# The first norm's factors: from column sums and a trip through memory to Newton steps on a row and 32x32 transpositions

## The chip, the cores and the metric

The kernel runs on one core of a Trainium2 chip. The metric is the device time of one execution in microseconds; the median of three runs is used. Times inside an execution come from the hardware profiler and count from the first instruction (the span).

## The reference

Two layers of a decoder trunk are computed for 256 new prompt tokens and for 8 sample sequences of 8 tokens: T = 320 tokens of D = 1024 features, in float32. Every sub-layer starts with an RMS norm. What the change touches is the norm of the first sub-layer and its two readers, the halves u and v of the first projection:

```
def rmsnorm(x, g):
    x32 = x.astype(jnp.float32)
    y = x32 * lax.rsqrt(jnp.mean(x32 * x32, axis=-1, keepdims=True) + EPS)
    return (y * g.astype(jnp.float32)).astype(x.dtype)

h = rmsnorm(x, norm_mix_g[0])
...
    h = jax.nn.gelu(x @ w_in)          # x is the normed input, (T, 1024) @ (1024, 4096)
    u, v = jnp.split(h, 2, axis=-1)    # 2048 columns each
    ... layer norm of v over its columns, spatial gating of v in chunks of 128 tokens ...
    y = (u * mixed.reshape(bsz, s, D_A)) @ w_out
```

## The kernel before

**Layout.** Activations lie with features on the 128 partitions and tokens along the row (xT: 8 blocks of 128 features x 320 tokens). Each float32 operand of a large matmul is split in a high part of reduced precision and the rest (xh and xl, wh and wl), and three matmuls (high by high, high by low, low by high) give the product. Weights come by DMA into raw; ScalarE copies raw to wh (L181), VectorE subtracts to get wl (L182). Both have three buffers, so the split of a group of weights may run as soon as TensorE has left the group three before it. A group here is two blocks of 128 rows by 512 columns, 16 matmuls of 512 columns.

**The norm's factor.** A norm's factor of a token is one over the root of the mean square. The kernel multiplies by the norm's weights g ahead of the matmuls (norm_block), and by the factor behind them: the factor is needed only where the product is read.

**v first.** layer_a starts with v in four passes (q = 0 to 3) over 512 columns each. In a pass the tokens are the rows of the result: pv[0] and pv[1] hold the two prompt halves of 128 tokens, pvs the 64 sample tokens. pv comes from the PSUM pool psa (five banks of 128x512), pvs from the pool psm (three). v_gelu(q, pv) reads a pass: for each token half ScalarE applies GELU with the factor as a scale per partition (L457; column t of self.rc), VectorE takes statistics (L458); the sample tokens are first summed from two halves of pvs (L454, L455) and then treated alike (L459, L460). After pass 0 the squares of x are summed over the 8 blocks into acc, 128x320 (square_block, L238 to L242). In pass 1, after four of eight blocks, norm_cols() gives the factors as columns (token on the partition, self.rc is 128x3), and v_gelu(0) follows; v_gelu(1) stands at the end of pass 1.

**norm_cols.** Each 128 tokens of acc are multiplied by ones, two columns wide (tile pc); VectorE scales and adds EPS (ms, L267), GpSimd raises to the power -0.5 (rc, L268).

**The row.** u is computed after v, with tokens along the row, and is multiplied by the factors as a row that is the same on all partitions (self.rb, L557). Before the change this row is got through memory: GpSimd writes self.rc into the array sums in DRAM (L477); later one DMA brings sums back to all partitions (back_a), together with row sums of the spatial weights (row_sums, L407 to L409: GpSimd masks wn, VectorE reduces it to rs8, DMA to sums). sums_laid then has ScalarE copy the row into self.rb (norm_back, L282 and L283), and GpSimd lay out rsum (L418).

**A norm that stands in the kernel already.** The norms ahead of the two gated MLPs use norm_spread and norm_root: acc is split, two matmuls with ones (128x128) add it up over the partitions and leave the sum on all of them (tile pb, 128x320), and eleven VectorE operations on 128x320 make the factors: half (L321), a first guess by integer arithmetic (L322) and three Newton steps of three operations (L324 to L326).

**Order.** TensorE's instructions stay in program order. On the other engines the order is fixed when the kernel is built, by a list scheduler that takes what is ready; each engine then runs its instructions strictly in that order.

Of the kernel before, what the change touches and what calls it, by code (L numbers as in the profile page):

```python
# [10 lines left out]
F32 = mybir.dt.float32  # L11
# [6 lines left out]
P = 128  # L18
EPS = 1e-6
TINY = 1e-37  # L20
TP = 256
NB, NS = 8, 8
T = TP + NB * NS
# [4 lines left out]
NH = 8  # L28
DK = 128
DV = 256  # L30
# [10 lines left out]
class Net:  # L41
# [232 lines left out]
        self.nc.scalar.copy(self.spread(acc2), self.twice(self.acc[:, TP:]))  # L274
        return acc2

    def norm_back(self, rows):

        nc = self.nc
        rows = rows.rearrange("p (c t) -> p t c", t=3)  # L280
        self.rb = self.tp.tile([P, T], F32, tag="rb", name="rb", bufs=1)
        nc.scalar.copy(self.rb[:, :TP].rearrange("p (t c) -> p t c", c=P), rows[:, :2, :])  # L282
        nc.scalar.copy(self.rb[:, TP:], rows[:, 2, 64:])  # L283

    def norm_row(self):

# [85 lines left out]
    def layer_a(self):  # L372
        nc, tc, I, O = self.nc, self.tc, self.I, self.O
        with tc.tile_pool(name="ya", bufs=1) as yp, tc.tile_pool(name="la", bufs=1) as lp:
            yh = yp.tile([P, KA, T], F32R, name="yh_a")
            yl = yp.tile([P, KA, T], F32R, name="yl_a")
            v = lp.tile([P, 3, DA], F32, name="v_a")
# [5 lines left out]
            rsum = lp.tile([P, NH, P], F32, name="rs_a")  # L383
            wn = lp.tile([P, NH, P], F32, name="wn_a")
            rs8 = lp.tile([P, NH], F32, name="rs8_a")
# [5 lines left out]
            def load_ws():  # L391
                nc.sync.dma_start(ws, I["a_ws"])
                nc.sync.dma_start(wn, I["a_wsn"])
                nc.sync.dma_start(trit, I["trit"])
                nc.gpsimd.memset(wss, 0.0)
                for r, c in halves:
                    nc.sync.dma_start(wss[r, :, c], I["a_wss"])
                    nc.sync.dma_start(bdt[r], I["bdt"])
                nc.sync.dma_start(bs, I["a_bs"].to_broadcast([P, NH, P]))
                nc.sync.dma_start(self.wg, I["b_wg"])  # L400
                nc.gpsimd.tensor_tensor(self.wg, self.wg, self.xv[:, V_MIX + 8:V_MIX + 16].unsqueeze(2).to_broadcast([P, KD, 32]), op=MULT)
                nc.gpsimd.tensor_tensor(ws, ws, trit.unsqueeze(1).to_broadcast([P, NH, P]), op=MULT)
                for r, c in halves:
                    nc.gpsimd.tensor_tensor(wss[r, :, c], wss[r, :, c], bdt[r].unsqueeze(1).to_broadcast([64, NH, 64]), op=MULT)

            def row_sums():
                nc.gpsimd.affine_select(wn, wn, pattern=[[0, NH], [-1, P]], compare_op=ALU.is_ge, fill=0.0, base=0, channel_multiplier=1)  # L407
                nc.vector.tensor_reduce(rs8, wn, axis=mybir.AxisListType.X, op=ADD)
                nc.gpsimd.dma_start(I["sums"][:, 3 * P:].rearrange("o (t g) -> t (o g)", g=NH), rs8)  # L409

            def sums_back():
                back = lp.tile([P, 11 * P], F32, name="back_a")
                nc.gpsimd.dma_start(back, I["sums"].to_broadcast([P, 11 * P]))
                return back

            def sums_laid(back):
                self.norm_back(back[:, :3 * P])
                nc.gpsimd.tensor_copy(rsum, back[:, 3 * P:].rearrange("p (t g) -> p g t", g=NH))  # L418

            nc.gpsimd.memset(mv[:64, 2, :], 0.0)  # L420

# [15 lines left out]
            def columns(q, k, pv, wh, wl):  # L437

                if q == 0 and k < 2:
                    return first_rows(k, pv, wh, wl)  # L440
                xs = self.xx[:, k, TP:TP + P]
                for t in range(2):
                    xh, xl = self.tokens(self.xh[:, k, :], t), self.tokens(self.xl[:, k, :], t)
                    self.mm(pv[t], xh, wh, k == 0, False)
                    self.mm(pv[t], xl, wh, False, False)
                    self.mm(pv[t], xh, wl, False, k == KD - 1)
                self.mm(pv[2], xs, wh, k == 0, False)
                self.mm(pv[2], xs, wl, False, k == KD - 1)

            def v_gelu(q, pv):  # L450
                cs = slice(q * 512, (q + 1) * 512)
                r = slice(64, P)
                vs = lp.tile([P, 512], F32, tag="vs", name="vs", bufs=2)[r]
                nc.scalar.copy(vs, pv[2][:64])  # L454
                nc.vector.tensor_tensor(vs, vs, pv[2][r], op=ADD)  # L455
                for t in range(2):
                    nc.scalar.activation(v[:, t, cs], pv[t], AF.Gelu_apprx_tanh, scale=self.rc[:, t:t + 1])  # L457
                    nc.vector.bn_stats(st[:, t, q, :], v[:, t, cs])  # L458
                done = nc.scalar.activation(v[r, 2, cs], vs, AF.Gelu_apprx_tanh, scale=self.rc[r, 2:3])  # L459
                return done, nc.vector.bn_stats(st[r, 2, q, :], v[r, 2, cs])  # L460

            waiting = None
            for q in range(4):
                pv = [self.psa.tile([P, 512], F32, tag="pa", name="pv") for _ in range(2)] + \
                    [self.psm.tile([P, 512], F32, tag="pm", name="pvs")]
                k = 0
                while k < KD:
                    (wh, wl), kn = self.take()
                    wh, wl = [x.rearrange("p (k e) c -> p k (e c)", e=4) for x in (wh, wl)]
                    for i in range(kn):  # L470
                        if q == 0 and k + i + 1 < KD:
                            self.enter(k + i + 1)
                        columns(q, k + i, pv, wh[:, i, :], wl[:, i, :])
                    k += kn
                    if q == 1 and k == 4:
                        self.norm_cols()
                        nc.gpsimd.dma_start(I["sums"][:, :3 * P].rearrange("o (c t) -> c (o t)", t=3), self.rc)  # L477
                        v_gelu(0, waiting)
                    if q == 3 and k == 2:
                        gone = v_gelu(2, waiting)  # L480
                        with self.behind(*gone):
                            sums_laid(back)
                if q == 0:
                    with tc.issue_after(self.last_split.ins):
                        for m in range(KD):
                            self.square_block(m)
                if q == 1:
                    load_ws()
                if q == 2:
                    row_sums()  # L490
                if q == 2:
                    back = sums_back()
                if q in (1, 3):
                    v_gelu(q, pv)
                waiting = pv
# [56 lines left out]
            for b in range(16):  # L552
# [3 lines left out]
                t = lp.tile([P, T], F32, tag="ur", name="ur", bufs=2)  # L556
# [1058 lines left out]
```

## Time and profile before

| | us |
|---|---|
| median of three runs (930.15 to 930.83) | 930.79 |
| the profiled execution | 930.84 |
| its span | 929.1 |
| TensorE busy (matmul) | 923.3 |
| VectorE busy | 692.3 |
| ScalarE busy | 507.5 |
| GpSimd busy | 113.1 |

The four passes of v take about the first 64 us of the span, and u the following 65. In the lines of the timeline the first two numbers are start and duration in us, then come the engine, the line of the kernel, the operation, what is written and what is read with shapes, and in brackets the idle time of the engine before it with what ended it. PE is TensorE's matmul, DVE VectorE, ACT ScalarE, POOL GpSimd.

### The profile page before, as it was taken

How to read it: one execution, taken by the hardware profiler on the slowest of the kernel's cores; microseconds unless marked ns; L12 is line 12 of the kernel's file. 1: busy time of each engine (PE TensorE's matmuls, PEld its weight loads, DVE VectorE, ACT ScalarE, POOL GpSimd, SP SyncE). 2: the span in 40 equal slices, each digit the busy share in tenths (PEclk: the TensorE clock that was granted, in tenths of full speed). 3: DMA queues.
4: the chain of work that ended last, by engine and by line, in shares of the span. 5: the costliest groups of instructions: out<-in, count | busy, mean ns of one | idle time of the engine just before them, and what ended most of it. 6: DMA issues, size and time to landing. Idle time of an engine off the chain costs nothing.

```text
span 929.1 us, 16828 instructions
## 1 busy us (share of the span) xinstructions
PE 923.3 (99%) x6268; PEld 894.2 (96%) x6268; DVE 692.3 (75%) x1299; ACT 507.5 (55%) x892; POOL 113.1 (12%) x312
## 2 busy tenths in 40 slices
PE   9999999999999999999999999999999999999997
PEld 8889999999999999998998989989999999999997
DVE  6667985597777764458999999798889777775551
ACT  7458544355544543336777786575655544544341
POOL 2400000011000000103221211001002110100001
PEclk9999999999999999999999999999999999999999
DMA  8866444444444445447688778775474444445642
GB/s 284 262 170 174 139 143 151 145 152 148 155 148 148 151 147 157 151 153 221 198 255 263 241 256 265 216 249 175 156 231 146 150 156 141 154 141 154 210 147 69
DMA packets 70625, 166.61 MB, mean 179 GB/s; under 512 B 12416, under 2 KB 31112, under 8 KB 70544
## 3 DMA queue, kind: packets, MB, share of 16 engines
q1 hardware_dynamic: 70336, 164.82, 56.9%
q8 instruction: 49, 0.80, 0.3%
q0 software_dynamic: 208, 0.73, 0.2%
q14 instruction: 32, 0.26, 0.1%
HBM read 149.20 MB, written 16.32 MB: 178 GB/s over the span
## 4 chain that ended last, share of the span: by engine, by line
PE 99%; DVEq 0%; DVE 0%; issue 0%
PE pm L50 78%; PE pv L50 10%; PE pvs L50 3%; PE num L50 2%; PE pyt L50 1%; PE pmix L50 1%; PE py L50 1%; PE psc L50 1%; PE pCp L50 1%; PE pcs L50 1%; PE pw L50 0%; PE pk L53 0%; PE pg L50 0%; PE pc L50 0%; PE pb L50 0%; PE pMb L50 0%
## 5 line engine op out<-in xcount | busy, mean ns | idle before, releaser
L181 ACT CAST wh<-raw 128x1024 fp32r<-128x1024 f32 (+4 forms) x252 | 254.8, 1012 | 278.4 <-PE pm L50 147.4
L182 DVE TENSOR_TENSOR wl<-raw,wh 128x1024 fp32r<-128x1024 f32 (+4 forms) x252 | 298.1, 1183 | 110.9 <-ACT wh L181 108.6
L50 PE MATMUL pm<-xh,wh 128*128 128x320 f32 x1088 | 338.3, 311 | 0.0
L50 PE MATMUL pm<-xh,wl 128*128 128x320 f32 x1088 | 336.2, 309 | 0.0
L50 PE MATMUL pm<-xl,wh 128*128 128x320 f32 x1088 | 336.1, 309 | 0.0
L50 PEld LDWEIGHTS pm<-xh,wh 128*128 128x128 f32 x1088 | 204.3, 188 | 1.7 <-ACT wh L181 0.5
L50 PEld LDWEIGHTS pm<-xl,wh 128*128 128x128 f32 x1088 | 204.3, 188 | 0.2
L50 PEld LDWEIGHTS pm<-xh,wl 128*128 128x128 f32 x1088 | 204.3, 188 | 0.0
L50 PE MATMUL pm<-yl_f,wh 128*128 128x320 f32 x308 | 95.1, 309 | 0.0
L50 PE MATMUL pm<-yh_f,wh 128*128 128x320 f32 x308 | 95.1, 309 | 0.0
L50 PE MATMUL pm<-yh_f,wl 128*128 128x320 f32 x308 | 95.1, 309 | 0.0
L50 PEld LDWEIGHTS pm<-yh_f,wl 128*128 128x128 f32 x308 | 57.9, 188 | 0.0
L50 PEld LDWEIGHTS pm<-yh_f,wh 128*128 128x128 f32 x308 | 57.9, 188 | 0.0
L50 PEld LDWEIGHTS pm<-yl_f,wh 128*128 128x128 f32 x308 | 57.9, 188 | 0.0
L602 DVE SCALAR_TENSOR_TENSOR fcv<-fpad,vecs,fcv 128x336 f32<-128x336 f32 x88 | 49.7, 564 | 1.5
L50 PE MATMUL pv<-wh,xh 128*128 128x512 f32 (+1 forms) x132 | 50.6, 389 | 0.0
L50 PE MATMUL pv<-wh,xl 128*128 128x512 f32 (+1 forms) x132 | 50.4, 387 | 0.0
L50 PE MATMUL pv<-wl,xh 128*128 128x512 f32 (+1 forms) x132 | 50.2, 386 | 0.0
L347 DVE TENSOR_TENSOR xT<-pm,xT 128x320 f32<-128x320 f32 x38 | 18.5, 489 | 30.5 <-PE pm L50 30.5
L50 PE MATMUL pm<-yhb,wh 128*128 128x320 f32 x128 | 39.6, 310 | 0.0
L50 PE MATMUL pm<-yh_a,wh 128*128 128x320 f32 x128 | 39.6, 309 | 0.0
L50 PE MATMUL pm<-yh_a,wl 128*128 128x320 f32 x128 | 39.5, 309 | 0.0
(354 smaller groups left out, 1446.2 us busy)
## 6 DMA issues: line engine op xcount, KB each, us to landing
raw<-in_f_up SPq DMA_DIRECT2D x88, 512.0 KB, 3.6
raw<-in_b_win SPq DMA_DIRECT2D x32, 512.0 KB, 4.2
raw<-in_f_dn SPq DMA_DIRECT2D x28, 448.0 KB, 3.4
C<-in_C SPq DMA_DIRECT2D x32, 258.0 KB, 4.7
raw<-in_a_win SPq DMA_DIRECT2D x16, 512.0 KB, 3.7
raw<-in_a_wo SPq DMA_DIRECT2D x16, 512.0 KB, 3.7
raw<-in_b_wv SPq DMA_DIRECT2D x16, 512.0 KB, 3.8
out_Cs<-C SPq DMA_DIRECT2D x32, 256.0 KB, 4.0
```

The lines of the kernel that those rows point to most:

```text
L50: self.pin(self.nc.tensor.matmul(out, lhsT, rhs, start=start, stop=stop))
L181: self.last_split = nc.scalar.copy(wh[:, c, :], raw[:, c, :])
L182: self.last_low = nc.vector.tensor_tensor(wl[:, c, :], raw[:, c, :], wh[:, c, :].bitcast(F32), op=SUB)
L347: self.last_sum = self.nc.vector.tensor_tensor(x, ps[:, :T], x, op=ADD)
L602: nc.vector.scalar_tensor_tensor(cv, pd[:, i:i + NC], self.vec(w + i * KF), cv, op0=MULT, op1=ADD)
```

## The change

norm_cols is no longer called in the first layer. acc is split after pass 0 (norm_spread), and at the place in pass 1 where norm_cols stood, norm_root gives the row of factors self.rb on all partitions. A new function root_cols makes the columns out of it: since the row is the same on every partition, the 32x32 transposition of the block of partitions 32g to 32g+31 and of tokens 32g to 32g+31 has in its first column the factors of these tokens. Six VectorE transpositions do this (for each of four blocks of partitions one for the two prompt halves, and two for the sample tokens). self.rc is then a strided view of the result. The trip of the row through DRAM and norm_back go, and the array sums keeps only the spatial weights' row sums.

```diff
-    def norm_back(self, rows):
-
-        nc = self.nc
-        rows = rows.rearrange("p (c t) -> p t c", t=3)
-        self.rb = self.tp.tile([P, T], F32, tag="rb", name="rb", bufs=1)
-        nc.scalar.copy(self.rb[:, :TP].rearrange("p (t c) -> p t c", c=P), rows[:, :2, :])
-        nc.scalar.copy(self.rb[:, TP:], rows[:, 2, 64:])
+    def root_cols(self):
+
+        cols = self.tp.tile([P, 3, 32], F32, tag="rcols", name="rcols", bufs=1)
+        for g in range(4):
+            r = slice(32 * g, 32 * g + 32)
+            self.nc.vector.transpose(cols[r, :2, :], self.rb[r, :TP].rearrange("p (t c) -> p t c", c=P)[:, :, r])
+            if g > 1:
+                self.nc.vector.transpose(cols[r, 2, :], self.tokens(self.rb[r], 2)[:, r])
+        self.rc = cols[:, :, 0]
...
-                nc.gpsimd.dma_start(I["sums"][:, 3 * P:].rearrange("o (t g) -> t (o g)", g=NH), rs8)
+                nc.gpsimd.dma_start(I["sums"].rearrange("o (t g) -> t (o g)", g=NH), rs8)
...
-                back = lp.tile([P, 11 * P], F32, name="back_a")
-                nc.gpsimd.dma_start(back, I["sums"].to_broadcast([P, 11 * P]))
+                back = lp.tile([P, NH * P], F32, name="back_a")
+                nc.gpsimd.dma_start(back, I["sums"].to_broadcast([P, NH * P]))
...
-                self.norm_back(back[:, :3 * P])
-                nc.gpsimd.tensor_copy(rsum, back[:, 3 * P:].rearrange("p (t g) -> p g t", g=NH))
+                nc.gpsimd.tensor_copy(rsum, back.rearrange("p (t g) -> p g t", g=NH))
...
                     if q == 1 and k == 4:
-                        self.norm_cols()
-                        nc.gpsimd.dma_start(I["sums"][:, :3 * P].rearrange("o (c t) -> c (o t)", t=3), self.rc)
+                        self.norm_root(*parts)
+                        self.root_cols()
                         v_gelu(0, waiting)
...
                         for m in range(KD):
                             self.square_block(m)
+                        parts = self.norm_spread()
```

More of the change, by code (lines that the diff above doesn't have):

```diff
@@ L1597 @@
     O = {k: nc.dram_tensor("out_" + k, s, F32, kind="ExternalOutput").ap() for k, s in _OUTS.items()}
-    for k, v in dict(rows=(8, 456), sums=(1, 11 * P), turn=(NH, P, 3 * DV), kturn=(NH, P, TP), frows=(P, 5 * T)).items():
+    for k, v in dict(rows=(8, 456), sums=(1, NH * P), turn=(NH, P, 3 * DV), kturn=(NH, P, TP), frows=(P, 5 * T)).items():
         I[k] = nc.dram_tensor(k, v, F32, kind="Internal").ap()
```

## The prediction

> **What bounds the kernel now.** I read the page first: its span, and the chain of work that ended last.
>
> ```profile
> span 929.1 us, 16828 instructions
> ...
> PE 99%; DVEq 0%; DVE 0%; issue 0%
> ```
>
> TensorE carries 99% of the chain. A microsecond of VectorE, ScalarE or GpSimd work is therefore worth nothing unless TensorE waits for it, and every wait that is put into TensorE's stream is lost for good. So I asked two things: what the change does to TensorE's own work, and whether something that TensorE needs comes later.
>
> Next I read the timeline of TensorE around the place of the edit (start, duration, then the instruction).
>
> ```profile
> 27.44 0.72 PE L50 MATMUL pc<-ones,acc 128*128 128x2 f32 x6
> 28.02 0.48 PE L50 MATMUL pv<-wh,xh 128*128 128x512 f32 x1
> 28.34 0.40 PE L50 MATMUL pv<-wh,xl 128*128 128x512 f32 x1
> ...
> 35.38 0.39 PE L50 MATMUL pv<-wh,xh 128*128 128x512 f32 x1
> ...
> 36.06 0.39 PE L50 MATMUL pv<-wh,xh 128*128 128x512 f32 x1
> ```
>
> At 27.44 stand the column sums of the norm, in the middle of the second of four passes over the columns of v (q = 1). At 35.38 the third pass (q = 2) begins with the tokens' first half; three matmuls later, at 36.06, it turns to the second half. Three steps in 0.68 us are 0.227 us a matmul of 512 columns: the stream is unbroken. Both times are deadlines. The pool psa has five banks: two hold pass 0, two hold pass 1, and the fifth serves the norm's sum. When pass 2 begins, one bank is free and the other comes back only when v_gelu(0) has read pass 0's first bank. v_gelu(0) needs the norm's factors as columns of tokens (self.rc).
>
> **The change part by part.**
>
> TensorE's own work. Removed are the six rows of pc: from 27.44 to 28.34 stand these and one matmul of v, so they cost 0.90 - 0.23 = 0.67 us. Added are the two matmuls of ones with the split sums of squares. The same two stand in the next layer's norm:
>
> ```profile
> 190.38 0.31 PE L50 MATMUL pb<-acc_h,ones 128*128 128x320 f32 x1
> 190.53 0.31 PE L50 MATMUL pb<-acc_l,ones 128*128 128x320 f32 x1
> 190.68 0.31 PE L50 MATMUL pm<-xh,wh 128*128 128x320 f32 x1
> ```
>
> They hold the stream for 190.68 - 190.38 = 0.30 us. TensorE gains 0.37 us, and the deadlines move to 35.01 (first bank) and 35.69 (second).
>
> VectorE around it, by its timeline:
>
> ```profile
> 25.22 1.23 DVE L182 TENSOR_TENSOR wl<-raw,wh 128x1024 fp32r<-128x1024 f32 x1 [0.29 <-ACT wh L181]
> 28.20 0.16 DVE L267 TENSOR_SCALAR ms<-pc 128x3 f32<-128x3 f32 x1 [1.75 <-PE pc L50]
> ...
> 35.03 1.22 DVE L408 TENSOR_REDUCE rs_a<-wn_a 128x8 f32<-128x1024 f32 x1 [0.99 <-POOL wn_a L407]
> 36.17 1.28 DVE L458 BATCH_NORM_STATS2 st_a<-v_a 128x6 f32<-128x512 f32 x2
> 37.48 0.69 DVE L455 TENSOR_TENSOR vs<-vs,pvs 64x512 f32<-64x512 f32 x1
> ```
>
> and ScalarE's:
>
> ```profile
> 27.41 1.05 ACT L181 CAST wh<-raw 128x1024 fp32r<-128x1024 f32 x1 [2.22 <-PE pvs L50]
> 29.37 1.27 ACT L457 ACTIVATE v_a<-pv,rc 128x512 f32<-128x512 f32 x2 [0.92 <-POOL rc L268]
> ...
> 31.73 1.05 ACT L181 CAST wh<-raw 128x1024 fp32r<-128x1024 f32 x1 [0.34 <-PE pvs L50]
> ...
> 35.84 0.58 ACT L454 COPY vs<-pvs 64x512 f32<-64x512 f32 x1
> ```
>
> Before, the factors are there at 29.37, one VectorE and one GpSimd operation behind the sums, so the first GELU of pass 0 ends at about 30.05 (half of that row), 6.0 us ahead of 36.06. That 6.0 us is all the cover there is for the new chain.
>
> The split of the sums (ScalarE's copy, VectorE's subtraction) goes into idle time: ScalarE is idle for 2.22 us up to 27.41, VectorE from 25.22 + 1.23 = 26.45 on. One subtraction of about 0.5 us (as 128x320 rows further down take) ends there near 26.9; TensorE wants it at 27.59. Cost nothing; without that cover, as much as it is late.
>
> The Newton chain. Before, the first reader of pc starts at 28.20, 0.04 us after the last row of pc (27.44 + 0.72). With the second new matmul at 27.59 and 0.31 us long, the chain starts at 27.94. Its eleven VectorE operations on 128x320 stand in the next layer's norm:
>
> ```profile
> 191.87 0.48 DVE L321 TENSOR_SCALAR half<-pb 128x320 f32<-128x320 f32 x1
> ...
> 194.32 0.49 DVE L324 TENSOR_TENSOR root<-rb,half 128x320 f32<-128x320 f32 x1
> 194.73 1.22 DVE L182 TENSOR_TENSOR wl<-raw,wh 128x1024 fp32r<-128x1024 f32 x1
> 195.87 0.48 DVE L325 TENSOR_TENSOR root<-root,rb 128x320 f32<-128x320 f32 x1
> ...
> 197.97 0.49 DVE L326 SCALAR_TENSOR_TENSOR rb<-root,rb 128x320 f32<-128x320 f32 x1
> 198.38 1.22 DVE L182 TENSOR_TENSOR wl<-raw,wh 128x1024 fp32r<-128x1024 f32 x1
> ```
>
> From 191.87 to 198.46 (197.97 + 0.49) are 6.59 us, of which one weight split takes 195.87 - 194.73 = 1.14; the chain alone is 5.45 us. The rows show more than the price: the order on VectorE is fixed beforehand, and wherever a step waits for the step ahead of it, other work that is ready gets in between. That is what costs here, since v's passes have three things that become ready while the chain runs:
>
> - the split of the weights whose wh runs at 27.41: ready at 28.46, 1.14 us;
> - the split whose wh runs at 31.73 behind a TensorE release (0.37 us earlier now): ready at about 32.4, 1.14 us. The chain then ends at 27.94 + 5.45 + 2.28 = 35.67;
> - the reduction of the spatial weights' rows at 35.03, which waits for GpSimd:
>
> ```profile
> 32.82 2.18 POOL L407 TENSOR_SCALAR_AFFINE_SELECT wn_a<-wn_a 128x1024 f32<-128x1024 f32 x1 [2.38 <-DMA wn_a<-in_a_wsn]
> ```
>
> It is ready at 35.00, which the edit doesn't move (the GpSimd power and DMA issue that go away stood ahead of it, and it waited for a DMA). 35.00 is before 35.67, so I count it: 1.14 us (36.17 - 35.03), chain end 36.81. Behind it the sum vs of pass 1 (the row at 37.48, 0.69 us) or a third weight split (1.14 us) may be ready by then too: ScalarE's two operations that feed them, vs and wh, start when pass 1 ends near 35.0 and take 0.58 and 1.05 us.
>
> The transpositions. None of 32x64 or 32x32 is in the trace; the nearest, in groups by shape (last numbers: busy us and mean ns of one):
>
> ```profile
> L1218 DVE STREAM_TRANSPOSE tb<-hn 128x768 f32<-128x768 f32 x7 | 6.8, 974 | 2.1 <-ACT hn L1213 2.0
> L1096 DVE STREAM_TRANSPOSE kb<-qs 128x256 f32<-128x256 f32 x6 | 2.6, 433 | 0.0
> ```
>
> A straight line through them, 1.06 ns an element and 0.16 us each, gives four of 0.23 and two of 0.20 us, 1.3 us in sum. Work that doesn't depend on the last row starts 0.08 us before its end (197.97 to 198.38), which makes 0.9 us for the six. Bounds: 0.4 us (elements alone) and 2.6 us (six times 0.43). I take 0.9, since the intercept is measured twice on this operation.
>
> Then the GELU, half of 1.27 to 0.69 us with its end, and a hop of 0.05 us on each side: 0.8 us. The second bank is free at 36.81 + 0.9 + 0.8 = 38.5 against the deadline 35.69. TensorE stalls for 2.8 us, gains 0.37, and the sum is +2.4 us; with vs in the chain as well, +3.1. I can't tell by 0.1 us what the fixed order lets in, and take +2.8.
>
> What else moves, at no cost. The row of factors (rb) is now there long before its first reader; ScalarE's two copies from back_a go, in a stretch in which it waits for TensorE; one GpSimd DMA goes and the broadcast shrinks from 11 to 8 rows of 128, both long before their readers. Behind the waiting GELU on ScalarE stand the splits of later weights. If the wh of 31.73 keeps its place behind the GELU, as it stands now, it would end near 41.5 and its low half near 42.7, for weights that TensorE reaches after eight plus eight matmuls (3.63 us) behind a start that is itself late, near 41.8: up to another 1 us. If it goes ahead, as readiness says, nothing.
>
> **The sum.** The profiled execution took 930.84 us beside a span of 929.1; the median is 930.79, so the two are the same within 0.05. 930.8 + 2.8 = **933.6 us**.
>
> **Rivals.**
>
> *Two splits alone get into the chain* (the fixed order puts the reduction behind). Chain end 35.67, bank free at 37.4, stall 1.7, net +1.3: 932.1 us. For it: the reduction is ready only 0.7 us ahead of the end. Against it: any step's gap will do.
>
> *Not slower: the chain is covered.* The 6.0 us of cover holds the chain if nothing is let in: chain end 27.94 + 5.45 = 33.4, bank free at 35.1, ahead of 35.69, and the saving of 0.37 is left: 930.4 us. It decides at a chain end of 35.69 - 0.8 - 0.9 = 34.0; a single split (34.5) already gives a stall of 0.5 and 931.0. For it: the split of 27.41 isn't needed before 35.0 and could wait. Against it: in the quoted norm a split stands inside the chain and another directly at its end.
>
> *The stall slows the clock.* TensorE's first matmuls on data step slowly:
>
> ```profile
> 6.37 0.63 PE L50 MATMUL pv<-wh,xl 128*128 128x256 f32 x2
> 6.80 0.50 PE L50 MATMUL pv<-wl,xh 128*128 128x256 f32 x2
> ```
>
> Two of 256 columns take 0.43 us here; later 512 columns take 0.227. From 4.07 us (when data came) to 6.80 that is 2.7 us at about half pace, 1.3 us lost. If the stall brings that back, and is at 3.5 us, the time is 930.8 - 0.4 + 3.5 + 1.3 = 935.2. The Trainium skill (TensorE: Matmul & The Clock Gate, section "What's actually happening") says that the clock halves after at least one idle window of some 3.4 us; by that rule a stall of 2.8 us does not pay it and one that fills a window does. No run here shows it, since TensorE has no such gap before.
>
> **How the numbers follow.** This kernel's measurement can tell about 0.2% (1.9 us) from no change. The reduction, with or without one more short operation, in the chain: 0.50 (933.2 to 934.4). Two splits alone: 0.24. Covered or nearly so: 0.14. A third split, a late wh or the slower clock on top: 0.12 (934.5 and more). The range 931.0 to 935.2 leaves out the fully covered case and the far end. The likeliest case, the last and a part of the second rival (transpositions dearer than taken, up to +1.7 by their bound) lie above 932.65: slower 0.65. Faster by 1.9 us has no source: TensorE can gain 0.37 us in all; 0.02. Same 0.33.
>
> **What the profile after would show.** pb at 27.4 on TensorE with 0.30 us to the next matmul; a gap in TensorE between the first three matmuls of pass 2 and the fourth, ended by ScalarE's GELU; eleven chain steps from 27.9 with two wl and the reduction between them; six transpositions of 0.2 us; the rest of the kernel later by one constant. I am wrong if both banks are free in time, if the transpositions or chain cost differently, or if a second wait follows in pass 2 or 3.

## The result and the profile after

The median went from 930.70 us (four runs, one more than in the table above) to 942.02 us (941.59 to 943.36): a ratio of 1.0123 [1.0108, 1.0138], 11.3 us slower where 2.8 were forecast. The direction was right, the size was not, and the range (to 935.2) missed it.

The chain that ended last (TensorE 99% before) now has a piece in which TensorE waits. First the waits of TensorE's queue after the change (engine, what it waited for: us, times, longest):

```profile
PE pv L50 <- ACT v_a L458: 9.6, 1, 9.6
```

Before, this view has nothing on the passes over v. The place, in TensorE's timeline after:

```profile
27.23 0.32 PE L50 MATMUL pb<-acc_h,ones 128*128 128x320 f32 x1
27.38 0.31 PE L50 MATMUL pb<-acc_l,ones 128*128 128x320 f32 x1
27.53 0.40 PE L50 MATMUL pv<-wh,xh 128*128 128x512 f32 x1
...
35.28 0.39 PE L50 MATMUL pv<-wl,xh 128*128 128x512 f32 x1
45.24 0.80 PE L50 MATMUL pv<-wh,xh 128*128 128x512 f32 x1 [9.58 <-ACT v_a L458]
45.84 0.63 PE L50 MATMUL pv<-wh,xl 128*128 128x512 f32 x1
...
50.90 0.39 PE L50 MATMUL pv<-wh,xh 128*128 128x512 f32 x1
```

The two matmuls of ones cost 0.30 us, and the gap lies where it was looked for: behind the first three matmuls of pass 2, ended by the GELU that frees the second bank. The next matmul is due at 35.28 + 0.23 = 35.51 and starts at 45.24: 9.7 us. Then 13 matmuls take 50.90 - 45.24 = 5.66 us instead of 13 x 0.227 = 2.95: another 2.7 us. The busy time by stretch shows why (columns: the stretch, its length and TensorE, TensorE loads, VectorE, ScalarE, GpSimd busy with counts; then granted clock, share of the DMA engines, GB/s):

```profile
35.50:45.24 9.74, 0.17 (x1) 0.00 (x0) 8.96 (x15) 1.67 (x4) 6.08 (x5) 0.76 0.57 170
45.24:50.90 5.66, 5.66 (x13) 4.47 (x14) 3.94 (x6) 3.31 (x6) 1.79 (x1) 0.51 0.49 129
```

The granted clock is 0.51 behind the gap; before, the same view reads 1.00 in all the passes over v. It reads 1.00 from 4.07 to 6.80 us too, where the prediction's rows show half pace, so the step from matmul to matmul is the surer sign. With the 0.4 us saved in TensorE's work this makes 12.0 of the 12.5 us by which the profiled execution (943.36) is longer than the one before; the remaining 0.5 I can't place, and the other three runs are 1.1 to 1.8 us shorter than the profiled one.

Why the GELU came so late: VectorE after,

```profile
27.73 0.49 DVE L323 TENSOR_SCALAR half<-pb 128x320 f32<-128x320 f32 x1 [1.09 <-PE pb L50]
28.28 1.23 DVE L182 TENSOR_TENSOR wl<-raw,wh 128x1024 fp32r<-128x1024 f32 x1
...
31.88 1.27 DVE L327 TENSOR_TENSOR root<-root,rb 128x320 f32<-128x320 f32 x1
33.07 3.42 DVE L182 TENSOR_TENSOR wl<-raw,wh 128x1024 fp32r<-128x1024 f32 x1
36.41 1.55 DVE L328 SCALAR_TENSOR_TENSOR rb<-root,rb 128x320 f32<-128x320 f32 x1
37.88 1.21 DVE L410 TENSOR_REDUCE rs_a<-wn_a 128x8 f32<-128x1024 f32 x1
39.01 0.48 DVE L326 TENSOR_TENSOR root<-rb,half 128x320 f32<-128x320 f32 x1
39.52 0.49 DVE L327 TENSOR_TENSOR root<-root,rb 128x320 f32<-128x320 f32 x1
39.93 1.22 DVE L182 TENSOR_TENSOR wl<-raw,wh 128x1024 fp32r<-128x1024 f32 x1
41.06 1.59 DVE L328 SCALAR_TENSOR_TENSOR rb<-root,rb 128x320 f32<-128x320 f32 x1
42.68 0.69 DVE L456 TENSOR_TENSOR vs<-vs,pvs 64x512 f32<-64x512 f32 x1
43.39 0.73 DVE L282 STREAM_TRANSPOSE rcols<-rb 32x64 f32<-32x64 f32 x3
```

and GpSimd after:

```profile
31.58 1.22 POOL L409 TENSOR_SCALAR_AFFINE_SELECT wn_a<-wn_a 128x1024 f32<-128x1024 f32 x1 [16.65 <-DMA wn_a<-in_a_wsn]
32.77 2.63 POOL L404 TENSOR_TENSOR ws_a<-ws_a,trit 128x1024 f32<-128x1024 f32 x1
35.48 2.13 POOL L406 TENSOR_TENSOR wss_a<-wss_a,bdt 64x512 f32<-64x512 f32 x1
39.39 0.79 POOL L411 DMA_DIRECT2D sums<-rs_a  x1 [1.78 <-DVE rs_a L410]
40.25 2.02 POOL L406 TENSOR_TENSOR wss_a<-wss_a,bdt 64x512 f32<-64x512 f32 x1
```

Read the two side by side. Three weight splits, the reduction and vs did get in ahead of the transpositions, one split more than forecast. But four rows are also longer than the same operation elsewhere: 1.27, 1.55 and 1.59 for 0.49, and 3.42 for 1.22, in sum 5.1 us. Each of them begins while a GpSimd operation runs and ends 0.35 us (the short ones) or 1.1 us (the split) behind its end: 32.80 and 33.15, 35.40 and 36.49, 37.61 and 37.96, 42.27 and 42.65. That is somewhat less than the operation's time alone (0.49 and 1.22), counted from the end of GpSimd's. Where GpSimd waits (37.61 to 39.39) or issues a DMA (39.39 to 40.18), the rows have 0.48 and 0.49.

### The profile page after: what moved, and what is told of

Same layout as the page of the kernel before. It is cut to its first block, busy times and chain, and to the rows that moved or that the text cites. A ratio compares the mean times of both kernels' runs of the same rounds, so it can differ in the third digit from the quotient of the medians.

```text
span 941.7 us, 16832 instructions
## 1 busy us (share of the span) xinstructions
PE 925.9 (98%) x6264; PEld 895.7 (95%) x6264; DVE 702.2 (75%) x1316; ACT 507.0 (54%) x891; POOL 112.2 (12%) x310
## 4 chain that ended last, share of the span: by engine, by line
PE 97%; DVE 1%; DMA 0%; ACT 0%; issue 0%; SPq 0%; POOLq 0%; POOL 0%; ACTq 0%
PE pm L50 77%; PE pv L50 8%; PE pvs L50 3%; PE num L50 2%; PE pyt L50 1%; PE pmix L50 1%; PE py L50 1%; PE psc L50 1%; DVE wl L182 1%; PE pcs L50 1%; PE pCp L50 0%; DMA wss_a<-in_a_wss 0%; PE pw L50 0%; DVE rb L328 0%; DVE vs L456 0%
## 5 line engine op out<-in xcount | busy, mean ns | idle before, releaser
L50 PEld LDWEIGHTS pv<-wh,xh 128*128 128x128 f32 x132 | 25.5, 196 | 15.1 <-ACT v_a L458 10.0
L50 PE MATMUL pm<-ylb,wh 128*128 128x320 f32 x128 | 39.5, 309 | 0.0
```

Of the source, the lines that this page charges most:

```text
L50: self.pin(self.nc.tensor.matmul(out, lhsT, rhs, start=start, stop=stop))
```

## The experiments

SBUF and PSUM are the two on-chip memories that hold this kernel's tiles, PSUM those that matmuls write. The helper behind() makes the instructions under it follow the given ones in the order that is fixed when the kernel is built.

Theory A: a VectorE operation with two operands in SBUF stands still until a running GpSimd operation that reads SBUF ends. Rival B: the rows are long because of the weights' DMAs. Rival C: only what got in between costs.

**e1, GpSimd idle during the chain.**

```diff
+            def mask_ws():
...
                         self.root_cols()
+                        mark = lp.tile([P, 1], F32, name="mark")
+                        marked = nc.gpsimd.tensor_copy(mark, self.rc[:, 0:1])
...
-                    row_sums()
+                    with self.behind(marked):
+                        mask_ws()
+                        row_sums()
```

mask_ws holds GpSimd's products of ws, wss and wg, which stood in load_ws.

> GpSimd's masking of the spatial weights, wg and wn is put behind a small GpSimd copy of the new factors' columns, so that GpSimd is idle while the Newton chain runs. Theory A (a VectorE operation with two operands in SBUF stands still until a running GpSimd operation ends): the rows of the chain go back to 0.49 us and the weight split from 3.42 to 1.2 us, the chain ends near 35.6 instead of 42.7, the second bank is free near 37.5 against 35.5, TensorE stalls for about 2.0 us instead of 9.7 and keeps its clock: 930.7 - 0.4 + 2.0 = 932.4 us. Rival B (the rows are long for another reason, such as the weights' DMAs, which fill the DMA engines at the time): rows of 1.2 to 3.4 us stay, the stall stays over 6 us, 938 us or more.

Measured 932.68 us, ratio 1.0019 [1.0010, 1.0028]. VectorE's timeline in e1:

```profile
31.90 1.22 DVE L182 TENSOR_TENSOR wl<-raw,wh 128x1024 fp32r<-128x1024 f32 x1
33.03 0.48 DVE L328 SCALAR_TENSOR_TENSOR rb<-root,rb 128x320 f32<-128x320 f32 x1
33.55 0.49 DVE L326 TENSOR_TENSOR root<-rb,half 128x320 f32<-128x320 f32 x1
34.08 0.49 DVE L327 TENSOR_TENSOR root<-root,rb 128x320 f32<-128x320 f32 x1
34.60 0.49 DVE L328 SCALAR_TENSOR_TENSOR rb<-root,rb 128x320 f32<-128x320 f32 x1
```

and the stretch of the chain, columns as above:

```profile
27.30:35.10 7.80, 7.80 (x35) 6.22 (x34) 7.43 (x13) 2.31 (x3) 0.00 (x0) 1.00 1.06 275
```

Every row is back to its quiet time although the DMA engines are full (1.06); after the change the rows were long where these were filled less (0.59 from 31.88 to 42.65 us). B falls. TensorE waits 1.7 us and keeps its clock (1.00 in the 6 us behind the wait, too). Since the reduction and a third split left the chain along with GpSimd's work, e1 alone doesn't say how much of the 9.3 us that it wins back (942.02 to 932.68) is due to the stretched rows; e2 keeps GpSimd's work there and takes most of the rest out.

**e2, GpSimd as it is, other VectorE work behind the transpositions.**

```diff
-                self.nc.vector.transpose(cols[r, 2, :], self.tokens(self.rb[r], 2)[:, r])
+                self.turned = self.nc.vector.transpose(cols[r, 2, :], self.tokens(self.rb[r], 2)[:, r])
...
-                    (wh, wl), kn = self.take()
+                    with self.behind(*([self.turned] if q == 2 and k < 4 else [])):
+                        (wh, wl), kn = self.take()
...
-                    row_sums()
+                    with self.behind(self.turned):
+                        row_sums()
```

> GpSimd's work stays where it is, but two of the three weight splits, the reduction and the sum vs are put behind the transpositions on VectorE, so that only one split is left in the chain. Theory A: the chain still meets the mask operations, each of which holds one of its steps up to its end: chain end near 39.5, stall near 6 us, with none to 2.7 us of slow clock behind it: 936 to 939 us. Rival C (what got in between is the whole cost, GpSimd is harmless): chain end 34.3, stall 0.7, 931.1 us.

Measured 938.86 us, ratio 1.0085 [1.0070, 1.0101]: C falls. In e2's VectorE timeline three steps still stand behind GpSimd:

```profile
33.39 1.27 DVE L326 TENSOR_TENSOR root<-rb,half 128x320 f32<-128x320 f32 x1
34.69 2.56 DVE L327 TENSOR_TENSOR root<-root,rb 128x320 f32<-128x320 f32 x1
37.28 1.44 DVE L328 SCALAR_TENSOR_TENSOR rb<-root,rb 128x320 f32<-128x320 f32 x1
```

These are 3.8 us over 3 x 0.49, and that is what TensorE waits beyond the 0.7 us that C gave: it idles for 4.49 us there, and that too is followed by the slow clock:

```profile
40.61:46.70 6.09, 6.09 (x14) 4.84 (x15) 5.89 (x8) 3.49 (x6) 0.00 (x0) 0.50 0.66 193
```

**e4, TensorE kept busy in the gap.**

```diff
+                    if q == 2 and k == 0 and t == 1:
+                        pd = self.psm.tile([P, 512], F32, tag="pm", name="pd")
+                        for _ in range(40):
+                            self.mm(pd, self.tokens(self.xh[:, 0, :], 0), wh, True, True)
```

> 40 matmuls of 512 columns, whose result nobody reads, fill TensorE's gap in pass 2 (40 x 0.227 = 9.1 of some 9.7 us). The chain stays as late. If the 13 matmuls behind the gap are slow because the gap lowered the clock: they run at 0.227 instead of 0.427 us, the granted clock stays 1.0, and the time falls by about 2.6 us to 939.4. If they are slow for another reason: 942 as before, or more.

Measured 939.79 us, ratio 1.0096 [1.0082, 1.0109]: 2.2 us less than the changed kernel's 942.02, with 40 matmuls more. In e4's timeline the matmuls behind the gap step by 0.23 us, and the granted clock reads 1.00 there (46 to 52 us):

```profile
44.85 0.39 PE L50 MATMUL pv<-wh,xl 128*128 128x512 f32 x1
45.08 0.40 PE L50 MATMUL pv<-wl,xh 128*128 128x512 f32 x1
```

So the slow matmuls are the gap's consequence, as the third rival had it. The Trainium skill (TensorE: Matmul & The Clock Gate, section "What's actually happening") puts the half clock behind an idle window of some 3.4 us: gaps of 9.58 and 4.49 us paid it and one of 1.71 didn't, which agrees.

**e3, a spare bank.**

```diff
-                pv = [self.psa.tile([P, 512], F32, tag="pa", name="pv") for _ in range(2)] + \
-                    [self.psm.tile([P, 512], F32, tag="pm", name="pvs")]
+                pv = [self.psa.tile([P, 512], F32, tag="pa", name="pv") for _ in range(1 if q == 2 else 2)]
+                if q == 2:
+                    pv.append(self.psm.tile([P, 512], F32, tag="pm", name="pv"))
+                pv.append(self.psm.tile([P, 512], F32, tag="pm", name="pvs"))
```

> The second prompt half of pass 2 gets a bank of the pool psm, one of which is idle, instead of waiting for pass 0's bank. The chain, its stretched rows and all that gets in between stay. If the wait for this bank is the only way in which the change costs time: no gap in TensorE, no slow clock, only the saving in TensorE's own work: 930.7 - 0.4 = 930.3 us, same. If the late VectorE work makes a second wait (weights split too late, pass 3's banks): 1 us or more above 930.7.

Measured 931.57 us, ratio 1.0007 [0.9998, 1.0016]. The chain is as late as in the change (transpositions from 42.69), yet 10 of the 11 us are gone: the bank was where the lateness reached TensorE. It is neither of the two expected outcomes quite; a smaller second wait showed in TensorE's waits:

```profile
PE pv L50 <- DVE wl L182: 0.7, 1, 0.7
```

It stands at 50.39, in pass 3: two weight copies on ScalarE, placed behind the six GELUs that waited for the late columns, start at 47.88 only.

**e6, e1 and e3 together** (both diffs).

> e1 and e3 together: a spare bank for pass 2, and GpSimd idle during the chain. e3 lost 0.7 us in pass 3, where weight splits stood on ScalarE behind GELUs that waited for the late columns. With columns some 7 us earlier that wait goes too, and only TensorE's saving is left: 930.8 - 0.4 = 930.4 us. If it is the spare bank itself that costs e3's 0.7 us: 931.5.

Measured 930.76 us, ratio 1.0003 [0.9994, 1.0012], and TensorE waits nowhere in v's passes. e3's rest was thus the late columns, not the bank. The saving of 0.4 us in TensorE's work, inside the interval, does not show: this version equals the kernel before and does not beat it.

**e5, e1 and e2 together** (both diffs).

> e1 and e2 together: GpSimd idle during the chain, and one weight split in it instead of two. By e1's rows the chain then ends one split (1.14 us) earlier, at 33.95, and the second bank is free 1.14 us sooner: of the stall, some 1.9 to 2.1 us in e1, 0.8 to 0.9 is left: 932.68 - 1.14 = 931.5 us. If the chain's end were not what TensorE waits for, e1's 932.7 would stay.

Measured 932.87 us, ratio 1.0023 [1.0014, 1.0033]: a miss by 1.4. TensorE's waits in e5:

```profile
PE pv L50 <- DVE wl L182: 0.8, 1, 0.8
...
PE pv L50 <- ACT v_a L460: 0.8, 1, 0.8
```

The wait for the bank is the 0.8 us expected. The other is new: the splits put behind the chain now meet the masks put behind the chain:

```profile
35.69 4.58 DVE L182 TENSOR_TENSOR wl<-raw,wh 128x1024 fp32r<-128x1024 f32 x2
```

Two splits take 4.58 us instead of the 2.36 that two in a row take in e3. The contention was moved, not removed, and came back as a wait for weights.

**e7, the row alone.** Newton's row in pass 3, the columns by norm_cols as before.

```diff
-                        self.norm_root(*parts)
-                        self.root_cols()
+                        self.norm_cols()
                         v_gelu(0, waiting)
                     if q == 3 and k == 2:
+                        self.norm_root(*self.norm_spread())
...
-                        parts = self.norm_spread()
```

> Half of the change: the row of factors by Newton steps in pass 3 instead of the trip through memory, while the columns still come by norm_cols as before. If the columns behind the chain are the whole cost: TensorE has the two matmuls of ones more (0.30 us) and waits nowhere, 930.8 + 0.3 = 931.1 us, same. If Newton steps among v's passes cost as such, by the VectorE time they take from weight splits: 932 us or more.

Measured 931.16 us, ratio 1.0005 [0.9997, 1.0014], no wait in v's passes. The same eleven steps, with weight splits between them and GpSimd idle beside them, cost nothing that the time shows beyond the matmuls of ones (931.1 forecast) when nobody waits for them.

**e8, contention by itself.** The kernel before, with GpSimd work beside the two quiet Newton chains.

```diff
                         parts = self.norm_spread()
+                        scr = up.tile([P, 1024], F32, name=f"scr{l}")
+                        nc.gpsimd.memset(scr, 1.0)
+                        nc.gpsimd.tensor_copy(scr[:, :T], parts[0].bitcast(F32))
+                        for _ in range(7 if l else 3):
+                            if l:
+                                nc.gpsimd.memset(scr, 1.0)
+                            else:
+                                nc.gpsimd.tensor_tensor(scr, scr, scr, op=MULT)
```

> The kernel before, with work for GpSimd put beside the Newton chains of the norms ahead of the gated MLPs, where GpSimd is idle otherwise: a copy and three products of 128x1024 (read and write SBUF) in layer 0, seven fills of 128x1024 (write only) in layer 1; their results are not used. Theory A, that a VectorE operation with two operands in SBUF stands still while a GpSimd operation that reads SBUF runs: in layer 0 the steps of 0.49 us become up to 2 us and end 0.3 to 0.4 us behind a GpSimd operation, while the operations with one SBUF operand (half, the integer guess) or one in PSUM keep 0.48 and 0.33 us. In layer 1 the fills leave all at 0.49 if reading is what matters, and stretch them alike if any GpSimd operation does. Rival B (traffic of DMAs): no row changes. The time may rise by the chain's delay, 0 to 8 us.

One run, 931.88 us. VectorE and GpSimd in layer 0, beside the products:

```profile
190.54 2.91 DVE L182 TENSOR_TENSOR wl<-raw,wh 128x1024 fp32r<-128x1024 f32 x1 [0.46 <-PE pb L50]
193.37 0.48 DVE L321 TENSOR_SCALAR half<-pb 128x320 f32<-128x320 f32 x1
193.89 1.50 DVE L322 TENSOR_SCALAR rb<-half 128x320 int32<-128x320 int32 x1
195.42 2.10 DVE L324 TENSOR_TENSOR root<-rb,half 128x320 f32<-128x320 f32 x1
```

```profile
190.48 6.70 POOL L638 TENSOR_TENSOR scr<-scr 128x1024 f32<-128x1024 f32 x3
```

and in layer 1, beside fills from 692.93 to 700.01:

```profile
694.16 0.48 DVE L321 TENSOR_SCALAR half<-pb 128x320 f32<-128x320 f32 x1
694.68 0.39 DVE L322 TENSOR_SCALAR rb<-half 128x320 int32<-128x320 int32 x1
695.11 0.49 DVE L324 TENSOR_TENSOR root<-rb,half 128x320 f32<-128x320 f32 x1
```

Beside the products the weight split took 2.91 us and the one step with two operands in SBUF 2.10; the step ends 0.34 us behind the last product (197.52 and 197.18). Fills leave the steps at 0.49, and the reader of PSUM keeps 0.48: A holds. One expectation failed: the integer guess, with a single operand in SBUF, went from 0.33 to 1.50 too. The Trainium skill (SBUF — State Buffer, section "Who interferes with whom") tells this: two SBUF inputs contend with a GpSimd operation that reads SBUF, and tensor_scalar may run in a mode that takes both ports. e8 agrees with the first. The guess's 1.50 us beside products fit the second; beside fills it took 0.39, a single instance, and the mode itself no row shows.

## Why the prediction was right or wrong

- **Where and by what way: right.** Bank, GELU and chain of factors were named; deadline 35.5 (35.69 forecast), chain start 27.7 (27.94). TensorE's own saving was 0.4 at the place, but in no median.
- **The chain's own price: right.** e1: 35.09 - 27.34 - 2 x 1.14 = 5.47 us (5.45).
- **What gets in between: right in kind, short by one split.** Both items that I left open, a third split (1.1) and vs (0.7), got in; in e1 both stand behind the transpositions. One reading was off without changing this count: the reduction was ready at 32.80, not at 35.00 (GpSimd's L407 in the kernel before, L409 after).
- **The step that failed: "Its eleven VectorE operations on 128x320 stand in the next layer's norm".** I took their price, and the 1.14 us of a split, from a place where GpSimd idles and put them beside GpSimd's masks. This left out 5.1 us. With the third split (1.1), vs (0.7) and the transpositions (0.3) it makes up, to within 0.5 us, the 6.7 us by which the second bank came later than forecast (45.24 instead of 38.5). The rows that tell of it were in the kernel before, in VectorE's and GpSimd's timelines around 47 us:

```profile
47.32 2.26 DVE L182 TENSOR_TENSOR wl<-raw,wh 128x1024 fp32r<-128x1024 f32 x1 [2.36 <-ACT wh L181]
```

```profile
46.34 2.16 POOL L418 COPY rs_a<-back_a 128x1024 f32<-128x1024 f32 x1 [3.79 <-DMA back_a<-sums]
```

  This split ends at 49.58, 1.08 us behind GpSimd's 48.50. I had read GpSimd's rows for when they make the reduction ready, not for what they hold up. The row of GpSimd that I did quote, 2.18 us at 32.82, shows the same the other way round: it starts beside a weight split of the kernel before, ends 0.97 us behind it, and takes 1.10 us in e7, where no such VectorE operation runs beside it.

```profile
32.81 1.22 DVE L182 TENSOR_TENSOR wl<-raw,wh 128x1024 fp32r<-128x1024 f32 x1 [0.71 <-ACT wh L181]
```

```profile
31.61 1.10 POOL L409 TENSOR_SCALAR_AFFINE_SELECT wn_a<-wn_a 128x1024 f32<-128x1024 f32 x1 [2.31 <-DMA wn_a<-in_a_wsn]
```

- **The slow clock: right as a mechanism, too small in chance and size.** It came with the longer gap and cost 2.7 us in the profile (e4: 2.2 in the median), not 1.3. I took the loss from the first data matmuls; 14 matmuls of ones run ahead of them (from 0.84 us on), so these may show only the rest of a slow stretch, which no run settles.
- **Transpositions: 1.18 us (43.39 to 44.57), not 0.9.** A small miss: from row to row they step by some 0.17 to 0.22 us, where 0.9 for six meant 0.15.
- **A late wh behind the GELUs: not the one named.** That one went ahead of the GELU (31.17) and cost nothing. Two later ones made TensorE wait 0.7 us in e3, once the larger wait was gone.

## What to carry to other kernels

Take an operation's price from rows that run beside the same neighbours as the place it moves to, and lay the GpSimd timeline over every VectorE chain that someone waits for. When a late result hurts, find the one resource through which it reaches the bound engine: here one spare PSUM bank returned 10 of 11 us, against 9.3 for the best shortening of the chain (e1). And price a gap of some microseconds on TensorE with the slow matmuls behind it.

## What the runs showed of the hardware that I had not expected

A VectorE operation with two operands in SBUF that began while a GpSimd operation that reads SBUF ran ended 0.35 us (128x320) or 1.1 us (128x1024) behind GpSimd's end, here up to 2.2 us late. GpSimd waits in turn: its select took 2.18 us instead of 1.10 beside a weight split. A one-operand integer tensor_scalar was held up too (1.50 for 0.33 us), while tensor_reduce (1.22 beside GpSimd's product from 34.98 us in the kernel before, 1.21 with GpSimd waiting after the change), a reader of PSUM (0.48) and everything beside fills hardly changed. TensorE gaps of 4.5 and 9.6 us were followed by 13 or 14 matmuls at a granted clock of 0.50 to 0.51, a gap of 1.7 us by none.
